# Every engine's instructions in program order, squares summed on POOL and gate rows combined on wide tiles, in a one-core mLSTM and convolution layer

## The chip, the cores and the metric

One core of a Trainium2 chip runs the whole kernel: TensorE (PE) for matmuls, VectorE (DVE), ScalarE (ACT), GpSimd (POOL), and SyncE (SP), which issues every DMA here. The metric is device microseconds of one execution. The version before takes 1819.15 us in the median of three runs (1818.57 to 1821.37).

## What is computed

One layer of a hybrid decoder, in float32, for 2048 tokens of width 1024:

```python
h = rms_norm(x, g_pre)
proj = jnp.einsum('bsd,de->bse', h, w_in)
q, k, v, o, z_m, i_pre, f_pre, u, gate_b, gate_c, z_c = jnp.split(
    proj, _split_points(), axis=-1)
...
log_i = i_pre + b_i
log_f = jax.nn.log_sigmoid(f_pre + b_f)
hm = mlstm_chunkwise(qh, kh, vh, log_i, log_f)
hm = group_rms_norm(hm, g_head, N_MLSTM_HEADS, x.dtype)
y_m = jax.nn.silu(z_m) * jax.nn.sigmoid(o) * hm
conv = causal_depthwise_conv(gate_c * u, conv_w)
y_c = jax.nn.silu(z_c) * group_rms_norm(gate_b * conv, g_conv, N_CONV_GROUPS, x.dtype)
out = jnp.einsum('bse,ed->bsd', jnp.concatenate([y_m, y_c], axis=-1), w_out)
return x + rms_norm(out, g_post)
```

There are 4 mLSTM heads with two gates each (`i_pre`, `f_pre`: eight columns of the projection) and 16 groups of convolution channels.

## The kernel before

**Precision by splitting.** A float32 operand is split in a high part, a rounded copy made on ACT (`split_h`, L165), and a low part, the difference made on DVE (`split_l`, L168). A product is high×high, high×low and low×high: three matmuls (L275 to L277).

**Products.** The sequence is worked in two halves of 1024 tokens. For a half, the output columns are 32 pairs of 128-column blocks, and each pair is a 2×2 block product (two column blocks by two 512-token quarters, over two halves of the channels) done with seven products in place of eight. The seven token operands, `hops[0]` to `hops[6]` (tiles `hH`, `hL`), are sums and differences of the normed input, built once a half. The seven weight operands of a pair (tile `w`) are made from four loaded blocks (`wraw`) by additions on DVE (L217, L241); those sums (`s`) are stored in DRAM (`w_scr`) and loaded again for the second half. A product is 4 × 3 = 12 matmuls into one 128x512 bank of PSUM. The banks of a pair are `uX`, `uD` and `uY`, filled in the order XDYXYDY; between the products ACT copies banks (`evac`, L434, L437, L440), and `TAKE` functions hand the results on: q, k and v through DRAM (`cs` L289, `tr` L295, `v_scr`), and the gates, convolution (`conv_0`), its group norm (`group_stat`, `rstd` on POOL, L391 and L392) and its output (`take_zz`).

**Slots.** A slot is one product. `on(slot, fn)` and `later(d, fn)` enter side work in an agenda; `run_slot` calls what stands there, bank copies first, then weights, stores and the rest. The weights of product i are planned in `plan_weights`: the load (`w_load`, on SP) 8 slots ahead, the sum (`w_sum`) 5, the cast (`w_high`) 4, the subtraction (`w_low`) 3. mLSTM work (`plan_group`) comes in groups of two chunks, 16 groups a half, about every 11 slots: an ACT and DVE chain from the PE results `num` and `upd` over `rd`, `numsb` (L698), its squares (L699), `rstd` on POOL and a last scaling (L704). What the agenda gives is the order in which the program is written. The order in which each engine runs its instructions is then set by the framework's scheduler, which may move them within their data dependencies.

**Start.** `start` does pairs 0 and 1 of the first half with plain products over eight channel blocks (`plain`, tiles `uH`, `uL`, made unnormed by L846 and L847), since the norm of the tokens isn't known yet. Meanwhile it sums the squares (`square` on ACT, L854; `sum_up` on PE with a matrix of ones, L860), takes root (L863) and reciprocal (L866) into `rb`, norms the blocks (`norm`, L871), scales the plain results (`plain_take`, L911), and builds the hops (`diff`, `fill`). Gate columns are done there by `gate_weights` (the tile `wgt`), `gate_proj` (L476) and `gate_take`, which adds high and low rows, multiplies by the norm and adds the bias on tiles of 4 partitions (L483, L489, L490, L491) and stores rows to DRAM. `plan_gates` loads them later as 128x32 tiles.

**End.** At the last slots `wo_hop` loads and splits the output weights into the hop tiles and `y_even` the first mix tile; then come 16 token tiles of the output projection (`po`, L593 to L595).

Of the kernel before, what the change touches and what calls it, by code (L numbers as in the profile page):

```python
# [16 lines left out]
P = 128  # L17
# [46 lines left out]
def hybrid_layer_kernel(  # L64
# [16 lines left out]

    const = ctx.enter_context(tc.tile_pool(name="const", bufs=1))
# [8 lines left out]
    graw_scr = scratch("graw_scr", [NH, HT])  # L91
# [32 lines left out]
    gb = const.tile([NH, 2], F32, name="gb")  # L124
# [27 lines left out]
    def t5(name, dtype=F32):  # L152
        return tpool.tile([P, Q], dtype, tag="t5", name=name)
# [128 lines left out]
    def seg(qd):  # L282
        return slice(Q * qd, Q * qd + Q)
# [196 lines left out]
    def gate_take(hf, qd, bank, scale=None):  # L480
        for w in range(2):
            lo_ = t5("glo")[0:NH]
            nc.vector.tensor_copy(lo_, bank[64 * w + 32 : 64 * w + 36])  # L483
            r = t5("grow")[0:NH]
            if scale is None:
                nc.vector.scalar_tensor_tensor(
                    r, bank[64 * w : 64 * w + NH], gb[:, w : w + 1], lo_, ALU.add, ALU.add)
            else:
# [5 lines left out]
    def plan_gates(hf, s):  # L494
        W32 = HT * NH // P
        wide = lambda a: a.rearrange("h (c q) -> (h c) q", q=W32)
        f, e, d, s2, pz = (
            sm.tile([P, W32], F32, tag="g" + n, name="g" + n, bufs=1) for n in ("f", "e", "d", "s2", "p"))
        R = {}

        def load():
            nc.sync.dma_start(f, wide(graw_scr[hf]))
# [80 lines left out]
        for d_, fn in (  # L583
            (0, load), (2, decay), (4, log1p_0), (5, lambda: log1p_1((13, 11))), (6, lambda: log1p_1((9, 7))),
            (7, log1p_2), (10, rows_load), (12, rows_0), (13, rows_1), (14, rows_2), (15, rows_3),
            (16, rows_4), (17, rows_5), (19, cols), (20, cols_take),
        ):
            on(s + d_, fn)
# [228 lines left out]
    def start():  # L817
# [32 lines left out]
        ssq = {}  # L850
# [14 lines left out]
        def inverse(qd):  # L865
            nc.vector.reciprocal(rb[:, seg(qd)], rb[:, seg(qd)])  # L866
# [35 lines left out]
        def plain(n, ch, qd):  # L902
            bank = bank_("u")
            for half in range(2):
                for k in range(KH):
                    plain_k(bank, n, ch, qd, half, k)
            return bank

        def plain_take(n, ch, qd, bank):
            t = t5("u")  # L910
            nc.vector.tensor_tensor(t, bank, rb[:, seg(qd)], ALU.mult)  # L911
            kind, i = PAIRS[n]
            TAKE[kind](0, i, ch, qd, t, False)
# [14 lines left out]
        nc.sync.dma_start(gb, gate_bias.rearrange("o (w h) -> h (o w)", w=2))  # L928
# [7 lines left out]
        for half in range(2):  # L936
            for k in range(KH):
                b = 2 * half
                unscaled(b, k)
# [5 lines left out]
                sum_up(0, KH * half + k, square(b, k))  # L945
            run_slot()
        for q in range(4):
            weights(1, q)
        root(0)
        inverse(0)  # L950
        p1 = [plain(1, 0, 0)]
        for k in range(KH):
            unscaled(1, k)
        for ch in range(2):
            plain_take(0, ch, 0, banks[ch])
        run_slot()
        gate_weights()
        sqs = [square(1, k) for k in range(KH)]
        p1.append(plain(1, 1, 0))
        norm(0)  # L960
        run_slot()
        for k in range(KH):
            unscaled(3, k)
            sqs.append(square(3, k))
        gate = gate_proj(((U[0], 0), (U[2], 1)))
        for i in range(KT):
            sum_up(1, i, sqs[i])
        run_slot()
        fill(0, 0)
        root(1)  # L970
        norm(2)
        for ch in range(2):
            plain_take(1, ch, 0, p1[ch])
        p0 = [plain(0, 0, 1)]
        run_slot()
        inverse(1)
        norm(1)
        gate_take(0, 0, gate, rb[:, seg(0)])
        p0.append(plain(0, 1, 1))
        norm(3)  # L980
# [4 lines left out]
        p1 = [plain(1, 0, 1)]  # L985
        for ch in range(2):
            plain_take(0, ch, 1, p0[ch])
        fill(3, 2)
        run_slot()
        fill(6, 3)  # L990
        diff(3, 3, 0)
        p1.append(plain(1, 1, 1))
        run_slot()
        diff(2, 2, 3)
        gate = gate_proj(((U[1], 0), (U[3], 1)))
        plain_take(1, 0, 1, p1[0])
        run_slot()
        plain_take(1, 1, 1, p1[1])
        gate_take(0, 1, gate, rb[:, seg(1)])
        run_slot()  # L1000
        fill(2, 3)
        run_slot()
        fill(4, 0)
        run_slot()
        fill(5, 2)
        run_slot()
# [6 lines left out]

    def load_wo(e, w2):
        for half in range(2):
            raw = t5("wor")
            nc.sync.dma_start(raw, wout[e * P : (e + 1) * P, seg(half)])
            split(w2[:, 0, seg(half)], w2[:, 1, seg(half)], raw)
        wos[e] = (w2[:, 0], w2[:, 1])

    def wo_hop(e):
        j, part = divmod(e, 2)
        load_wo(e, hpool.tile([P, 2, DM], F32R, tag=f"h{j}{'HL'[part]}", name="wo"))

    def load_y(t, tile_):
        hf, tt = divmod(t, NC)
        ts = slice(tt * P, (tt + 1) * P)
        ys[t] = []
        for g in range(2):
            H, L = tile_(f"yH{g}"), tile_(f"yL{g}")  # L1030
            for half in range(2):
                r = tpool.tile([P, 4, P], F32, tag="t5", name="yr")
                es = slice(4 * half, 4 * half + 4)
                if g == 0:
                    for i in range(2):
                        nc.sync.dma_start(
                            r[:, 2 * i : 2 * i + 2, :],
                            h_scr[hf][2 * half + i, tt].rearrange("e p t -> p e t"))
                    gr = tpool.tile([P, 4, P], F32, tag="t5", name="gr")
                    nc.sync.dma_start(gr, g_scr[hf][es, :, ts].rearrange("e p t -> p e t"))  # L1040
                    nc.vector.tensor_tensor(r, r, gr, ALU.mult)
                else:
                    nc.sync.dma_start(r, y_scr[hf][es, :, ts].rearrange("e p t -> p e t"))
                split(H[:, es], L[:, es], r)
            ys[t] += [(H[:, i, :], L[:, i, :]) for i in range(8)]

    def y_even(t):
        tags = iter(("cv", "cv", "cu", "rb"))
        load_y(t, lambda name: c4(next(tags), name, [P, 8, P], F32R))
# [3 lines left out]
    OZ0 = 24 * NPROD  # L1053
    plan_weights()
# [5 lines left out]
    plan_gates(0, 15)  # L1060
    plan_gates(1, U + 9)
# [42 lines left out]
    while any(agenda.values()):  # L1104
        run_slot()
    ph1.close()
# [105 lines left out]
```

## Time and profile before

| | before |
|---|---|
| median of 3 runs | 1819.15 us (1818.57 to 1821.37) |
| profiled execution, its own time | 1826.05 us |
| its span, first to last instruction | 1824.3 us |
| mean granted clock of TensorE | 0.987 |
| busy: PE, DVE, ACT, POOL | 1764.4, 1153.4, 817.5, 94.1 us |
| moved by DMA | 278.18 MB |

All durations below come from the one profiled execution. In the views, "[4.45 <-ACT w L165]" is idle time of the engine just before an instruction, and what ended it; PEclk or clock is the granted clock as a share of 2.4 GHz. An average over the span says little here: the start, the stretches with mLSTM work, the convolution and the output projection have different limits, so the windows are to be read one by one.

### The profile page before, as it was taken

Reading aid. Unit: us, or ns where it says so; the run is one execution under the profiler, and the core shown is the slowest. Engines: PE = TensorE matmul, PEld = TensorE weight load, DVE = VectorE, ACT = ScalarE, POOL = GpSimd, SP = SyncE. Lnnn points to the kernel's source line nnn. Section 1 sums busy time; section 2 is a strip of 40 time slices with the busy share of each in tenths; the row PEclk is TensorE's granted clock in tenths of the full one; section 3 lists DMA queues with packets and bytes.
Section 4 is the critical chain, followed back from the end, with each engine's and each line's share of the span. In section 5 each row is a group of like instructions: output and inputs, shape, how many; then the busy total and the mean of one; then the engine's idle time right before and its main releaser. Section 6 shows DMA issues by size and latency. Waiting matters only on the chain.

```text
span 1824.3 us, 23028 instructions
## 1 busy us (share of the span) xinstructions
PE 1764.4 (97%) x7801; PEld 1420.6 (78%) x7801; DVE 1153.4 (63%) x2193; ACT 817.5 (45%) x1599; POOL 94.1 (5%) x106
## 2 busy tenths in 40 slices
PE   8799889999999999999888999999999999999998
PEld 5577768888888878787666888888888888888887
DVE  7967459888878788844535867676756663333321
ACT  6334346655556555633334555564655541111110
POOL 0000001010101000000000101010100000000000
PEclk9999989999999999999999999999999999999999
DMA  6247557645455778656554545454455594334311
GB/s 209 43 127 181 132 153 219 194 152 160 138 168 164 209 242 267 220 144 157 137 123 128 152 122 151 115 152 122 136 156 145 179 298 147 115 116 120 111 53 40
DMA packets 358946, 278.18 MB, mean 152 GB/s; under 512 B 186724, under 2 KB 268908, under 8 KB 358828
## 3 DMA queue, kind: packets, MB, share of 16 engines
q1 hardware_dynamic: 358828, 276.71, 52.8%
q8 instruction: 61, 1.00, 0.2%
q14 instruction: 57, 0.47, 0.1%
HBM read 183.13 MB, written 93.49 MB: 152 GB/s over the span
## 4 chain that ended last, share of the span: by engine, by line
PE 79%; issue 12%; DMA 3%; DVE 3%; ACT 2%; SPq 1%; POOL 0%; DVEq 0%; ACTq 0%; POOLq 0%
PE uY L275 8%; PE uY L277 8%; PE uY L276 8%; PE po L594 7%; PE po L593 7%; PE po L595 6%; PE uX L277 5%; PE uX L275 5%; PE uX L276 5%; PE uD L275 5%; PE uD L277 5%; PE uD L276 5%; PE num L594 1%; PE num L595 1%; SPq L189 1%
## 5 line engine op out<-in xcount | busy, mean ns | idle before, releaser
L168 DVE TENSOR_TENSOR w<-wraw,w 128x512 fp32r<-128x512 f32 x410 | 279.0, 687 | 136.4 <-ACT w L165 135.4
L165 ACT CAST w<-wraw 128x512 fp32r<-128x512 f32 x410 | 249.9, 619 | 172.3 <-PE uY L277 81.8
L275 PE MATMUL uY<-hH,w 128*128 128x512 f32 x744 | 299.4, 402 | 21.3 <-ACT w L165 17.0
L277 PE MATMUL uY<-hH,w 128*128 128x512 f32 x744 | 297.0, 399 | 2.8 <-DVE w L168 2.8
L276 PE MATMUL uY<-hL,w 128*128 128x512 f32 x744 | 295.6, 397 | 0.0
L275 PE MATMUL uD<-hH,w 128*128 128x512 f32 x496 | 200.8, 405 | 11.8 <-ACT w L165 11.8
L275 PE MATMUL uX<-hH,w 128*128 128x512 f32 x496 | 199.2, 402 | 8.2 <-ACT w L165 8.2
L594 PE MATMUL po<-wo,yH 128*128 128x512 f32 (+1 forms) x528 | 205.5, 389 | 0.0
L593 PE MATMUL po<-wo,yH 128*128 128x512 f32 (+1 forms) x528 | 204.3, 387 | 0.0
L595 PE MATMUL po<-wo,yL 128*128 128x512 f32 (+1 forms) x528 | 203.7, 386 | 0.0
L277 PE MATMUL uD<-hH,w 128*128 128x512 f32 x496 | 200.5, 404 | 0.7 <-DVE w L168 0.7
L276 PE MATMUL uD<-hL,w 128*128 128x512 f32 x496 | 200.1, 403 | 0.0
L277 PE MATMUL uX<-hH,w 128*128 128x512 f32 x496 | 199.1, 401 | 0.8 <-DVE w L168 0.8
L276 PE MATMUL uX<-hL,w 128*128 128x512 f32 x496 | 198.4, 400 | 0.0
L275 PEld LDWEIGHTS uY<-hH,w 128*128 128x128 f32 x744 | 141.1, 190 | 59.1 <-ACT w L165 21.0
L277 PEld LDWEIGHTS uY<-hH,w 128*128 128x128 f32 x744 | 140.9, 189 | 40.1 <-DVE w L168 6.3
L276 PEld LDWEIGHTS uY<-hL,w 128*128 128x128 f32 x744 | 141.3, 190 | 31.9
L275 PEld LDWEIGHTS uD<-hH,w 128*128 128x128 f32 x496 | 95.5, 193 | 34.2 <-ACT w L165 12.6
L275 PEld LDWEIGHTS uX<-hH,w 128*128 128x128 f32 x496 | 94.4, 190 | 31.9 <-ACT w L165 10.5
L593 PEld LDWEIGHTS po<-wo,yH 128*128 128x128 f32 x528 | 99.2, 188 | 23.0 <-DVE c L449 0.4
L595 PEld LDWEIGHTS po<-wo,yL 128*128 128x128 f32 x528 | 99.2, 188 | 21.5
L594 PEld LDWEIGHTS po<-wo,yH 128*128 128x128 f32 x528 | 99.3, 188 | 20.9
(198 smaller groups left out, 2589.1 us busy)
## 6 DMA issues: line engine op xcount, KB each, us to landing
wraw<-in_wt_dram SPq DMA_DIRECT2D x226, 256.0 KB
wraw<-w_scr SPq DMA_DIRECT2D x120, 256.0 KB
w_scr<-wraw SPq DMA_DIRECT2D x90, 256.0 KB
v_scr<-tr SPq DMA_DIRECT2D x128, 64.0 KB
vraw<-v_scr SPq DMA_DIRECT2D x32, 256.0 KB
h_scr<-hT SPq DMA_DIRECT2D x128, 64.0 KB
y_scr<-sg SPq DMA_DIRECT2D x32, 256.0 KB
g_scr<-c SPq DMA_DIRECT2D x32, 256.0 KB
```

The source lines that it names most:

```text
L165: nc.scalar.copy(dH, src)
L168: nc.vector.tensor_tensor(dL, src, dH.bitcast(F32), ALU.subtract)
L189: later(d, lambda: nc.sync.dma_start(dst, src), STORE)
L275: nc.tensor.matmul(bank, wH[:, k, :], bH[:, k, :], start=first, stop=False, **kw)
L276: nc.tensor.matmul(bank, wH[:, k, :], bL[:, k, :], start=False, stop=False, **kw)
L277: nc.tensor.matmul(bank, wL[:, k, :], bH[:, k, :], start=False, stop=stop and k == KH - 1, **kw)
L593: nc.tensor.matmul(out_, aH, bH, start=start, stop=False)
L594: nc.tensor.matmul(out_, aH, bL, start=False, stop=False)
L595: nc.tensor.matmul(out_, aL, bH, start=False, stop=stop)
```

## The change

1. `in_order`, called at the end of every slot, chains each instruction to the one written before it on the same engine (PE, DVE, ACT, POOL, SP) by an order-only dependency. Through the two input halves each engine then runs what the agenda wrote, in that order. The output stage behind it isn't chained.
2. Squares: of 8 squared tiles of a quarter 7 are added on POOL (L889), and one ones-matmul follows (L893) where 8 stood.
3. Gate rows: `gate_take` copies the bank with ACT (L503) and stores four strips of 4 rows; `plan_gates` loads them as 128x32 tiles, together with the reciprocal norms (`r_scr`), and combines them there in a new step; later steps move by a slot or two.
4. `start` is written in another order: squares of the first quarter before the blocks of the second, `inverse` and `norm` earlier, `gate_weights` after the first hop, v's transposes put off to later slots, some differences from other blocks, and the last hops spread over more slots.
5. Output weights (`plan_wo`) and the first mix tile (`y_parts`) are loaded some slots before they are split, and spread over more slots.

```diff
+    def in_order(start=False):
+        ins = nc.cur_bb.bb.instructions
+        n = traced.pop("n", 0)
+        for i in ins[n:]:
+            if i.engine not in ENGINES:
+                continue
+            prev = traced.get(i.engine)
+            if prev is not None and not start:
+                tc.add_manual_dep(
+                    i, prev,
+                    mybir.DependencyInfo(mybir.DependencyClass.NoSync, mybir.DependencyReason.DATA),
+                    reason="in_order")
+            traced[i.engine] = i.name
+        traced["n"] = len(ins)
...
         clock[0] += 1
+        in_order()
...
-    def gate_take(hf, qd, bank, scale=None):
-        for w in range(2):
-            lo_ = t5("glo")[0:NH]
-            nc.vector.tensor_copy(lo_, bank[64 * w + 32 : 64 * w + 36])
...
-                nc.vector.tensor_tensor(r, bank[64 * w : 64 * w + NH], lo_, ALU.add)
-                nc.vector.tensor_tensor(r, r, scale[0:NH], ALU.mult)
-                nc.vector.tensor_scalar(r, r, gb[:, w : w + 1], None, ALU.add)
-            nc.sync.dma_start((graw_scr[hf] if w else gate_scr[hf][0])[:, seg(qd)], r)
+    def gate_take(hf, qd, bank):
+        t = t5("graw")[0:GW]
+        nc.scalar.copy(t, bank)
+        for i in range(4):
+            store(graw_scr[hf][i][:, seg(qd)], t[32 * i : 32 * i + NH])
...
+        def combine():
+            for w, t in enumerate((li, f)):
+                hi, lo = R["raw"][:, 2 * w], R["raw"][:, 2 * w + 1]
+                if scaled:
+                    nc.vector.tensor_tensor(t, hi, lo, ALU.add)
+                    nc.vector.tensor_tensor(t, t, R["r"], ALU.mult)
+                    nc.vector.tensor_scalar(t, t, gb[:, w : w + 1], None, ALU.add)
+                else:
+                    nc.vector.scalar_tensor_tensor(t, hi, gb[:, w : w + 1], lo, ALU.add, ALU.add)
+            store(wide(gate_scr[hf][0]), li)
...
             nc.scalar.activation(sq, raw(b, k)[:, 0], AF.Square)
-            return sq
-
-        def sum_up(qd, i, sq):
-            if i == 0:
-                ssq[qd] = ps.tile([P, Q], F32, tag="g", name="ssq")
-            nc.tensor.matmul(ssq[qd], ones, sq, start=i == 0, stop=i == KT - 1)
+            qd = b % 2
+            if qd not in acc:
+                acc[qd] = sq
+            else:
+                nc.gpsimd.tensor_tensor(acc[qd], acc[qd], sq, ALU.add)
+
+        def sum_up(qd):
+            ssq[qd] = ps.tile([P, Q], F32, tag="g", name="ssq")
+            nc.tensor.matmul(ssq[qd], ones, acc[qd], start=True, stop=True)
...
+        weights(1, 0)
+        weights(1, 1)
+        for half in range(2):
+            for k in range(KH):
+                square(2 * half, k)
+        weights(1, 2)
+        weights(1, 3)
+        run_slot()
+        for b in (1, 3):
+            for k in range(KH):
+                unscaled(b, k)
+        p1 = [plain(1, 0, 0, lambda: sum_up(0))]
         root(0)
         inverse(0)
+        norm(0)
+        for b in (1, 3):
+            for k in range(KH):
+                square(b, k)
+        run_slot()
+        p1.append(plain(1, 1, 0))
         for ch in range(2):
             plain_take(0, ch, 0, banks[ch])
+        norm(2)
+        fill(0, 0)
         gate_weights()
         run_slot()
         gate = gate_proj(((U[0], 0), (U[2], 1)))
+        sum_up(1)
+        gate_take(0, 0, gate)
         root(1)
+        inverse(1)
+        norm(1)
+        run_slot()
...
-    on(2 * U - 3 * NPROD, lambda: y_even(0))
-    for j in range(NPROD):
-        for part in range(2):
-            on(2 * U - NPROD + j + 1, lambda e=2 * j + part: wo_hop(e))
+    for i, (load, go) in enumerate(y_parts(0, even_tile())):
+        on(2 * U - 3 * NPROD + 2 * i, load)
+        on(2 * U - 3 * NPROD + 2 * i + 3, go)
+    for e in range(2 * NPROD):
+        plan_wo(e)
```

ACT, near the first two-chunk group of mLSTM work (about 200 us in the profile before). A row is line, operation and output and input tiles; "x4" is four in a row. Before:

```order
L289 COPY cs<-uY 128x512
L165 CAST cH<-state_112 128x258
L698 ACTIVATE numsb<-num,rd 128x256
L699 ACTIVATE num,hss<-numsb 128x256
L704 ACTIVATE numsb<-numsb,hss 128x256 x2
L165 CAST w<-s_1571 128x512
L434 COPY uY<-uX 128x512
L165 CAST w<-wraw 128x512 x4
```

The same place in the change (L185 is the cast of before's L165, L728, L729 and L734 are its L698, L699 and L704, L310, L455 and L461 its bank copies L289, L434 and L440):

```order
L185 CAST cH<-state_113 128x258
L728 ACTIVATE numsb<-num,rd 128x256
L729 ACTIVATE num,hss<-numsb 128x256
L653 ACTIVATE R<-R 128x256
L461 COPY u_1780<-uY 128x512
L185 CAST w<-wraw 128x512
L310 COPY cs<-uX 128x512
L185 CAST w<-s_1785 128x512
L185 CAST kH<-kT 128x256
L185 CAST qH<-tmp 128x256
L185 CAST w<-wraw 128x512
L734 ACTIVATE numsb<-numsb,hss 128x256 x2
```

Before, L704 stands right behind L699 and four weight casts are gathered further on; in the change three weight casts, one a slot, stand between L729 and L734.

DVE in the start, from the scaling of the first plain results to behind the second reciprocal. Before:

```order
L911 TENSOR_TENSOR u<-u,rb_164 128x512 x2
L483 COPY glo<-gate 4x512
L168 TENSOR_TENSOR hL_592<-xs,hH_591 128x1024
L489 TENSOR_TENSOR grow<-gate,glo 4x512
L483 COPY glo<-gate 4x512
L490 TENSOR_TENSOR grow<-grow,rb_164 4x512
L866 RECIPROCAL rb_164<-rb_164 128x512
L491 TENSOR_SCALAR grow<-grow,gb 4x512
```

In the change, from the first reciprocal on (L899 is before's L866, L904 its L871, L946 its L911, L188 its L168; L485 clears the gate weights):

```order
L899 RECIPROCAL rb_165<-rb_165 128x512
L904 SCALAR_TENSOR_TENSOR xs<-xs,gp,rb_165 128x512 x4
L946 TENSOR_TENSOR u<-u,rb_165 128x512 x2
L904 SCALAR_TENSOR_TENSOR xs<-xs,gp,rb_165 128x512 x4
L188 TENSOR_TENSOR hL_429<-xs,hH_428 128x1024 x2
L485 CAST wgt<-zero 128x800
L489 TENSOR_TENSOR wgt<-wgraw,wgt 128x8x4 x2
L899 RECIPROCAL rb_165<-rb_165 128x512
```

The operations on 4 partitions are gone, and the gate weights, which stood at the head of DVE's program and ahead of the first reciprocal, stand between the two reciprocals.

## Rows read from the trace of the kernel before

**Rows 1.** The page, busy time of each engine over the span.

```profile
PE 1764.4 (97%) x7801; PEld 1420.6 (78%) x7801; DVE 1153.4 (63%) x2193; ACT 817.5 (45%) x1599; POOL 94.1 (5%) x106
```

**Rows 2.** Windows: length, busy PE, PEld, DVE, ACT, POOL, clock, DMA share, GB/s.

```profile
45.60:91.20 45.60, 35.18 (x139) 25.87 (x137) 44.90 (x59) 13.71 (x19) 0.00 (x0) 0.92 0.21 43
100.00:270.00 170.00, 156.58 (x665) 124.78 (x664) 99.22 (x198) 63.37 (x124) 2.05 (x4) 0.95 0.60 155
195.00:210.00 15.00, 10.55 (x40) 8.36 (x39) 8.29 (x17) 6.78 (x15) 0.90 (x2) 0.77 0.39 109
270.00:600.00 330.00, 330.00 (x1518) 270.59 (x1517) 281.19 (x564) 194.87 (x384) 38.28 (x38) 1.00 0.56 168
600.00:760.00 160.00, 156.56 (x706) 126.79 (x705) 131.79 (x236) 96.47 (x179) 7.83 (x8) 1.00 0.79 246
840.00:1000.00 160.00, 141.32 (x593) 107.86 (x593) 71.71 (x151) 59.09 (x125) 2.66 (x6) 0.96 0.57 138
```

**Rows 3.** Waits of PE: waited for, total us, times, longest us.

```profile
PE uD L275 <- ACT w L165: 11.8, 3, 4.5
```

**Rows 4.** Timeline near 200 us: start, us, engine, line, operation, tiles, [idle before].

```profile
199.81 0.91 ACT L704 ACTIVATE numsb<-numsb,hss 128x256 f32<-128x256 f32 x2 [1.11 <-POOL hss L392]
200.63 0.60 ACT L165 CAST w<-s 128x512 fp32r<-128x512 f32 x1
201.28 0.79 PE L275 MATMUL uD<-hH,w 128*128 128x512 f32 x1 [4.45 <-ACT w L165]
```

**Rows 5.** Timeline near 940 us, ACT, and SP's queue.

```profile
940.20 0.58 ACT L289 COPY cs<-uY 128x512 f32<-128x512 f32 x1 [6.96 <-PE uY L277]
...
946.30 0.62 ACT L165 CAST w<-wraw 128x512 fp32r<-128x512 f32 x1
...
939.47 2.18 SPq L189 DMA_DIRECT2D v_scr<-tr  x4
```

**Rows 6.** Timeline of the start: blocks, squares, their sum, reciprocals, first product.

```profile
16.16 2.76 ACT L846 ACTIVATE uH<-xs,gp 128x512 fp32r<-128x512 f32 x4
18.83 4.26 ACT L854 ACTIVATE xsq<-xs 128x512 f32<-128x512 f32 x8
...
31.34 3.35 DVE L866 RECIPROCAL rb<-rb 128x512 f32<-128x512 f32 x1 [3.46 <-ACT rb L863]
...
42.30 7.03 PE L860 MATMUL ssq<-xsq,ones 128*128 128x512 f32 x16
...
50.09 3.35 DVE L866 RECIPROCAL rb<-rb 128x512 f32<-128x512 f32 x1 [0.31 <-ACT rb L863]
...
89.21 0.80 PE L275 MATMUL uY<-hH,w 128*128 128x512 f32 x1 [10.42 <-ACT w L165]
```

**Rows 7.** Groups by line, DVE, 30 to 100 us: count, busy us, mean ns, idle.

```profile
L168 DVE TENSOR_TENSOR hL<-xs,hH 128x1024 fp32r<-128x1024 f32 (+1 forms) x16 | 16.7, 1072 | 0.0
L871 DVE SCALAR_TENSOR_TENSOR xs<-xs,gp,rb 128x512 f32<-128x512 f32 x16 | 11.1, 739 | 0.0
...
L483 DVE COPY glo<-gate 4x512 f32<-4x512 f32 x4 | 2.7, 687 | 0.2
L489 DVE TENSOR_TENSOR grow<-gate,glo 4x512 f32<-4x512 f32 x4 | 2.7, 682 | 0.1
L490 DVE TENSOR_TENSOR grow<-grow,rb 4x512 f32<-4x512 f32 x4 | 2.7, 672 | 0.0
L491 DVE TENSOR_SCALAR grow<-grow,gb 4x512 f32<-4x512 f32 x4 | 1.7, 436 | 0.0
```

**Rows 8.** POOL: a group of the start, then the timeline around 307 us.

```profile
masks.py:199 POOL TENSOR_SCALAR_AFFINE_SELECT ident<-ident 128x128 f32<-128x128 f32 x1 | 0.3, 292 | 0.0
...
306.64 2.90 POOL L392 TENSOR_TENSOR red<-red,mhalf 128x16 f32<-128x16 f32 x1
307.89 0.68 DVE L217 TENSOR_TENSOR s<-wraw 128x512 f32<-128x512 f32 x1
```

**Rows 9.** The chain of waits, a weight load's landing.

```profile
607.05 5.91 DMA wraw<-in_wt_dram
```

More of the change, by code (lines that the diff above doesn't have):

```diff
@@ L90, in hybrid_layer_kernel @@
     g_scr = scratch("g_scr", [8, P, HT])
-    graw_scr = scratch("graw_scr", [NH, HT])
+    graw_scr = scratch("graw_scr", [4, NH, HT])
+    r_scr = dram.tile([HT], F32, name="r_scr")
     gate_scr = scratch("gate_scr", [2, NH, HT])
@@ L499, in plan_gates @@
         R = {}
         def load():
-            nc.sync.dma_start(f, wide(graw_scr[hf]))
+            R["raw"] = sm.tile([P, 4, W32], F32, tag="graw", name="graww", bufs=1)
+            for i in range(4):
+                nc.sync.dma_start(R["raw"][:, i], wide(graw_scr[hf][i]))
+            if scaled:
+                R["r"] = sm.tile([P, W32], F32, tag="gr", name="gr", bufs=1)
+                for h in range(NH):
+                    nc.sync.dma_start(R["r"][h * W32 : (h + 1) * W32], r_scr.rearrange("(c q) -> c q", q=W32))
@@ L900, in plain_k, with plain @@
             nc.tensor.matmul(bank, wL[:, k, :], bH[:, k, :], start=False, stop=end)
-        def plain(n, ch, qd):
+        def plain(n, ch, qd, between=None):
             bank = bank_("u")
@@ L906, in plain @@
                     plain_k(bank, n, ch, qd, half, k)
+                if half == 0 and between:
+                    between()
             return bank
@@ L912, in plain_take @@
             kind, i = PAIRS[n]
-            TAKE[kind](0, i, ch, qd, t, False)
+            slow = NSTART + 2 * ch + qd - clock[0] if kind == "v" else 0
+            later(slow, lambda: TAKE[kind](0, i, ch, qd, t, False))
         load(0, 0)
@@ L937, in start @@
             for k in range(KH):
-                b = 2 * half
-                unscaled(b, k)
+                unscaled(2 * half, k)
                 if k == 0:
@@ L944, in start @@
                     plain_k(banks[ch], 0, ch, 0, half, k)
[L945 to L948, printed above, removed]
+        weights(1, 0)
[10 more added lines that the diff above has]
+        p1 = [plain(1, 0, 0, lambda: sum_up(0))]
         root(0)
         inverse(0)
-        p1 = [plain(1, 0, 0)]
-        for k in range(KH):
-            unscaled(1, k)
+        norm(0)
[4 more added lines that the diff above has]
+        p1.append(plain(1, 1, 0))
         for ch in range(2):
             plain_take(0, ch, 0, banks[ch])
+        norm(2)
+        fill(0, 0)
+        gate_weights()
         run_slot()
[L957 to L960, printed above, removed]
-        run_slot()
[L962 to L971, printed above, removed]
+        gate = gate_proj(((U[0], 0), (U[2], 1)))
+        sum_up(1)
+        gate_take(0, 0, gate)
+        root(1)
+        inverse(1)
+        norm(1)
+        run_slot()
+        p0 = [plain(0, 0, 1)]
+        nc.sync.dma_start(r_scr.rearrange("(o t) -> o t", o=1), rb[0:1, :])
         for ch in range(2):
             plain_take(1, ch, 0, p1[ch])
-        p0 = [plain(0, 0, 1)]
+        norm(3)
         run_slot()
-        inverse(1)
-        norm(1)
-        gate_take(0, 0, gate, rb[:, seg(0)])
         p0.append(plain(0, 1, 1))
-        norm(3)
         diff(0, 1, 0)
@@ L1005, in start @@
         fill(5, 2)
+        run_slot()
+        fill(6, 3)
+        run_slot()
         run_slot()
@@ L1012, in hybrid_layer_kernel, with wo_raw, wo_split, plan_wo @@
     wos, ys = {}, {}
+    def wo_raw(e, half, raw=None):
+        raw = raw or t5("wor")
+        nc.sync.dma_start(raw, wout[e * P : (e + 1) * P, seg(half)])
+        return raw
+    def wo_split(e, half, w2, raw):
+        split(w2[:, 0, seg(half)], w2[:, 1, seg(half)], raw)
+        wos[e] = (w2[:, 0], w2[:, 1])
     def load_wo(e, w2):
         for half in range(2):
[L1016 to L1021, printed above, removed]
-        j, part = divmod(e, 2)
-        load_wo(e, hpool.tile([P, 2, DM], F32R, tag=f"h{j}{'HL'[part]}", name="wo"))
-    def load_y(t, tile_):
+            wo_split(e, half, w2, wo_raw(e, half))
+    def plan_wo(e):
+        s = 2 * U - NPROD + 1 + 3 * e // 4
+        j, part = divmod(e, 2)
+        R = {}
+        def load():
+            for half in range(2):
+                R[half] = wo_raw(e, half, rawp.tile([P, Q], F32, tag="raw", name="wor"))
+        def go():
+            w2 = hpool.tile([P, 2, DM], F32R, tag=f"h{j}{'HL'[part]}", name="wo")
+            for half in range(2):
+                wo_split(e, half, w2, R[half])
+        on(s - 2, load)
+        on(s, go)
+    def y_parts(t, tile_):
         hf, tt = divmod(t, NC)
@@ L1029, in load_y @@
         for g in range(2):
-            H, L = tile_(f"yH{g}"), tile_(f"yL{g}")
+            R = {}
             for half in range(2):
-                r = tpool.tile([P, 4, P], F32, tag="t5", name="yr")
                 es = slice(4 * half, 4 * half + 4)
[L1034 to L1044, printed above, removed]
@@ L1045, in load_y, with load @@
-            ys[t] += [(H[:, i, :], L[:, i, :]) for i in range(8)]
+                def load(g=g, half=half, es=es, R=R):
+                    r = R[half] = tpool.tile([P, 4, P], F32, tag="t5", name="yr")
+                    if g == 0:
+                        for i in range(2):
+                            nc.sync.dma_start(
+                                r[:, 2 * i : 2 * i + 2, :],
+                                h_scr[hf][2 * half + i, tt].rearrange("e p t -> p e t"))
+                        R["g", half] = tpool.tile([P, 4, P], F32, tag="t5", name="gr")
+                        nc.sync.dma_start(R["g", half], g_scr[hf][es, :, ts].rearrange("e p t -> p e t"))
+                    else:
+                        nc.sync.dma_start(r, y_scr[hf][es, :, ts].rearrange("e p t -> p e t"))
@@ new lines, in go @@
+                def go(g=g, half=half, es=es, R=R):
+                    if half == 0:
+                        R["H"], R["L"] = tile_(f"yH{g}"), tile_(f"yL{g}")
+                    r = R[half]
+                    if g == 0:
+                        nc.vector.tensor_tensor(r, r, R["g", half], ALU.mult)
+                    split(R["H"][:, es], R["L"][:, es], r)
+                    if half == 1:
+                        ys[t].extend((R["H"][:, i, :], R["L"][:, i, :]) for i in range(8))
+                yield load, go
@@ L1047, in y_even, with load_y, even_tile @@
+    def load_y(t, tile_):
+        for load, go in y_parts(t, tile_):
+            load()
+            go()
+    def even_tile():
+        tags = iter(("cv", "cv", "cu", "rb"))
+        return lambda name: c4(next(tags), name, [P, 8, P], F32R)
     def y_even(t):
-        tags = iter(("cv", "cv", "cu", "rb"))
-        load_y(t, lambda name: c4(next(tags), name, [P, 8, P], F32R))
+        load_y(t, even_tile())
     U = NPAIR * NPROD
     OZ0 = 24 * NPROD
+    in_order(True)
     plan_weights()
```

46 lines of the change are left out of this document (21 added, 25 removed).

## The prediction

> **What bounds the kernel now.** The table of busy time shows TensorE (PE) at 1764.4 of 1824.3 us [rows 1]: the kernel gains only where PE stands still or runs at the lower of its two clocks, or where PE work goes. The windows tell where [rows 2]. Idle is the window less PE's busy time; clock loss is (1 − granted clock) × window, 1.00 being the 2.4 GHz level.
> - 45.6 to 91.2 us, the start: DVE busy 44.90 of 45.60 us. PE waits for it.
> - 100 to 270: 13.4 us idle, clock 0.95, so 8.5 us more: 21.9.
> - 270 to 600: no loss, though DVE is busy 281.19 of 330 us.
> - 600 to 760: 3.4 idle.
> - 840 to 1000: 18.7 idle, clock 0.96, so 6.4 more: 25.1, with DVE and ACT less than half busy.
>
> So in the middle no engine is full, yet PE waits. The waits of PE name ACT's cast of a weight block (L165) [rows 3]: three times for the bank uD, 4.5 us the longest, and likewise for uX and uY. The timeline around 200 us shows how [rows 4]: the cast stands on ACT directly behind L704, which waits 1.11 us for POOL at the end of a long mLSTM chain; the cast of 0.60 us then runs with PE already standing, 4.45 us. Around 940 us it is another neighbour [rows 5]: ACT waits 6.96 us for PE's product (the copy L289), and a cast that product order needs soon runs at 946.30, behind copies. Both are matters of the order in which ACT was told to work. A wait also lowers the clock afterwards: 195 to 210 us holds 4.45 us idle and a mean clock of 0.77, (1 − 0.77) × 15 = 3.45 us. One such miss costs 7.9 us.
>
> **The change, part by part.**
>
> *Program order.* In the written program a weight block is loaded 8 slots before its product, summed 5, cast on ACT 4 and subtracted on DVE 3 slots before. A product is 12 matmuls; at 330.00 us for 1518 [rows 2], 0.22 each with some shorter ones among them, it takes 2.6 to 2.8 us. So a cast gets some 11 us of lead. The ACT rows in the order of the change show it: casts now stand between the mLSTM pieces and ahead of L734, the old L704. A delay of 1.11 or 2 us is then covered by the three products ahead. The cover is gone if ACT or DVE gets over 8 us behind. I expect that in neither stretch and recover 0.9 of 21.9 + 25.1: **−42.3**; the ends are 0.5 (half the misses were late data, not order) and 1.0. At 600 to 760 us DVE is busy 131.79 of 160 us, so I take half of 3.4: **−1.7** (0 to −3.4). What can be late next is DVE: in program order it can't fetch light work out of the next slot where a slot is heavy. The zz pairs (8) put two group statistics and gates in some slots, some eleven operations of L217's 0.68 us [rows 8], 7.4 us of DVE against a 2.8 us product. A PSUM bank is needed again two products later, 5.6 us; 7.4 − 5.6 is under 2, and the weight lead takes part of it. Between 0 and 8 × 1.8 = 14 us; DVE at 281.19 of 330 without loss [rows 2] is nearer the low end: **+3**.
>
> *Squares.* Before, 16 ones-matmuls of two passes a sum: 7.03 us of PE each [rows 6]. One matmul remains of 8, so 7.03 × 7/8 = 6.2 us of PE go twice, and 7 POOL additions come for each sum. PE's part lies in the DVE-bound start, so it counts through the chain root, reciprocal, norm. No row has POOL adding 128x512. Bounds: 0.68 us, DVE's time for that shape (L217); above, the POOL row of 128x128 with one input, 0.292, four times the size and two inputs at double: 2.3 [rows 8]. I take 4 × 0.292 = 1.2, nearest to the POOL row. Squares follow at 0.53 us (4.26 for 8). They began at 18.83; written ahead of the four blocks of L846 (2.76 for 4) and two of the casts (0.62) that preceded them, they begin 4.0 earlier, at 14.8 us. The last addition ends at 15.9 + 7 × 1.2 = 24.3, the matmul (0.9) at 25.2. The root on ACT stands behind those two casts and 8 blocks (6.8 us), until 25.8. So the first reciprocal starts at about 26.5 instead of 31.34. At 2.3 it is 15.9 + 16.1 + 0.9 + 0.7 = 33.6, 2.3 us later than before.
>
> The Trainium skill, "GPSIMD Engine Reference", section "3.1 Elementwise — side-by-side cycle accounting", gives an fp32 addition 1.96 times DVE's time and says to keep elementwise work on DVE; an estimate from it is 1.96 × 0.68 = 1.33 us, 25.2 in place of 24.3, still hidden behind the root's wait for ACT.
>
> *Gate rows.* The four-partition operations (16, at 2.7 + 2.7 + 2.7 + 1.7 = 9.8 us [rows 7]) cost as much as full tiles and leave DVE; two copies on ACT (0.58 like L289) and eight stores come, later a few 128x32 operations in slots with room. Four of the 16 stood before the second reciprocal, 12 behind it (7.1 us).
>
> *Start reordered.* Between the reciprocals DVE now has 3.35, 8 × 0.69 (L871), two scalings at 0.68, 2 × 1.04 (hL, 16.7 for 16 [rows 7]) and the fill of the gate weights, which stood at the program's head: 800 wide, 0.8 by the 1024 of hL. Sum 13.1, so these are ready at 39.6. Only then can PE do the gate projection (16 × 0.22) and, behind it, the sum (0.9), ACT the root (0.7): 44.7, or 49.1 if the wait drops the clock to half. DVE stands 5.1 to 9.5 us for this **new wait**, with the norm of the second quarter behind it. The second reciprocal comes 1.0 to 5.4 us earlier than 50.09. From there to the first product before: 39.1 us. Less 7.1 gate operations, less three transposes put off (2.0), plus two scalings (1.4) and three hL (3.1) that stood elsewhere: 34.5. The first product starts at 79.2 to 83.6 in place of 89.21 [rows 6]; the products after it still wait for DVE's low halves, one after the other, so I count half of 5.6 to 10.0: **−4** (+8 with POOL at 2.3, −7 at the best).
>
> *Output weights and mix tiles* are loaded slots ahead: nothing, in the cover of PE's own products (L593 to L595 lose nothing above).
>
> **Sum**, against the profiled 1826.05: −42.3 − 1.7 + 3 − 4 = −45.0, so 1781.0. The median of the runs shown stands 6.9 lower. PE's full-clock work can't differ between executions; stalls can, and the change removes most, so half of the 6.9 counts: 1781.0 − 3.4 = 1778.
>
> **Rivals.**
> - *Waits move.* Half of 47 us stays, as misses in heavy DVE slots and as late sums: 1826 − 23.5 − 4 + 3 = 1801, less 3 to 6.9: 1795 to 1812. For: DVE at 281.19 of 330. Against: 270 to 600 loses nothing.
> - *POOL stands in DVE's way.* If an addition on POOL held DVE's two-input operations for its whole length, the seven of the second sum would cost DVE up to 7 × 1.2 = 8.4 us and those of the first, beside less DVE work, some 3: start +7, not −4, so 1789. Against: while POOL's L392 ran 2.90 us at 306.64, DVE's two-input L217 took its normal 0.68 [rows 8], though POOL read only 16 columns. The Trainium skill, "SBUF — State Buffer", section "🔬 SBUF: two separate sides", has such pairs block each other for whole instructions; the row just named speaks against it, at a small POOL operand.
> - *Slower: SP's queue in program order.* A store waits for its data, and loads behind it wait too. In the qk and v pairs four v_scr stores took 2.18 us of issue [rows 5], up to 12 issues stand in a slot, and their transposes depend on PE. Load to sum is three slots, 8.4 us; a landing took 5.91 [rows 9]. It decides when a load is issued over 2.5 us late. Each miss costs 7.9; 14 such pairs missing once in every second give 7 × 7.9 = 55, against −45: 1826 + 10 − 7 = 1829, a loss. Against: one slot's issues lag 3 us at most by the row's 0.55 each, and the next slots catch up.
> - *The order changes little*, since ACT's waits were for data: about 1819.
>
> **How the numbers follow.** About 3.6 us (0.2%) is what a measurement can tell. Forecast 0.57 (1760 to 1795), waits move 0.16, POOL in the way 0.08, little changes 0.04, slower 0.15. Faster is the first three: 0.81. The range goes from 1760 (middle fully regained, start −7: 1826 − 50 − 7 − 6.9 = 1762) to 1813 and leaves out the last two, 0.19.
>
> **What would show it.** Right: PE idle under 3 us at 100 to 270 and 840 to 1000 and granted clock 1.00; no PE wait on the weight cast over 1 us after the start; L893 twice, in place of 32 passes; first reciprocal at 26 to 28 us, second at 45 to 50, with DVE idle ahead of it. Wrong: PE waiting for DVE in the zz pairs; SP issuing weight loads late; POOL additions over 2 us, or DVE operations longer beside them. The forecast is wrong as a whole if PE's idle sum stays over 40 us.

## The result and the profile after

The change takes 1779.57 us in the median of four runs (1776.88 to 1782.27), against 1820.06 for the version before (1818.57 to 1821.37): a ratio of 0.9778, 95% interval 0.976 to 0.9796, some 40 us faster. The profiled execution took 1780.39 us (before: 1826.05), with a span of 1778.5. In one of the experiments below, the one with the gate weights early, one execution of four, the profiled one, took 3466.91 us; its ratio is from the other three and it has no rows here.

The page's busy time and the windows of the changed kernel, with the columns of [rows 2]:

```profile
PE 1735.6 (98%) x7773; PEld 1408.5 (79%) x7773; DVE 1153.6 (65%) x2175; ACT 820.9 (46%) x1608; POOL 121.3 (7%) x120
```

```profile
45.60:91.20 45.60, 33.76 (x132) 25.09 (x132) 37.69 (x44) 14.92 (x20) 0.00 (x0) 0.87 0.21 54
100.00:270.00 170.00, 170.00 (x769) 138.10 (x768) 118.28 (x244) 75.79 (x148) 2.64 (x4) 1.00 0.73 187
270.00:600.00 330.00, 328.52 (x1504) 268.64 (x1503) 276.74 (x544) 191.06 (x378) 45.52 (x38) 1.00 0.54 165
600.00:760.00 160.00, 158.41 (x712) 127.31 (x712) 134.40 (x231) 94.16 (x172) 5.80 (x8) 1.00 0.77 244
840.00:1000.00 160.00, 160.00 (x736) 131.05 (x735) 99.53 (x205) 78.47 (x164) 12.14 (x12) 1.00 0.60 149
```

The two stretches that held most of the loss have none now: PE is busy 170.00 of 170 and 160.00 of 160 us, at a granted clock of 1.00 ([rows 2] had 156.58 at 0.95 and 141.32 at 0.96). Where before lost nothing, 270 to 600 us, 1.5 us of idle is new. The start is the other way round: in 45.6 to 91.2 us DVE, which was busy 44.90 of 45.60, now stands for 7.9 us, and PE's clock is 0.87 in place of 0.92. PE's waits say where (waited for, total us, times, longest):

```profile
PE gate L497 <- DVE wgt L489: 10.5, 1, 10.5
...
PE uX L296 <- ACT w L185: 5.0, 1, 5.0
PE uX L298 <- DVE w L188: 4.3, 1, 4.3
PE ssq L893 <- POOL xsq L889: 3.7, 1, 3.7
PE uY L296 <- ACT uY L455: 3.5, 3, 1.5
```

The waits for the weight cast that [rows 3] listed are gone behind 100 us; the one of 5.0 us that is left lies at 86 us, in the start. ACT's timeline around 200 us answers to [rows 4]: a weight cast of 0.62 us now follows the bank copy of its own slot, and ACT waits for PE, not PE for ACT.

```profile
197.34 0.57 ACT L455 COPY uY<-uX 128x512 f32<-128x512 f32 x1 [1.71 <-PE uX L298]
197.82 0.62 ACT L185 CAST w<-wraw 128x512 fp32r<-128x512 f32 x1
198.42 0.62 ACT L185 CAST vH<-vraw 128x512 fp32r<-128x512 f32 x1
201.22 0.59 ACT L458 COPY p<-uD 128x512 f32<-128x512 f32 x1 [2.18 <-PE uD L298]
201.70 0.62 ACT L185 CAST w<-wraw 128x512 fp32r<-128x512 f32 x1
```

Where the time went is seen best by counting products, which both programs do in the same number. A product here is twelve matmuls with a hop operand; the count begins behind the plain products of the start. The first matmul of the fifth product and that of the 289th, in before:

```profile
101.65 0.39 PE L275 MATMUL uY<-hH,w 128*128 128x512 f32 x1
...
1020.32 0.40 PE L275 MATMUL uD<-hH,w 128*128 128x512 f32 x1
```

The same two in the change:

```profile
104.71 0.40 PE L296 MATMUL uY<-hH,w 128*128 128x512 f32 x1
...
969.13 0.39 PE L296 MATMUL uD<-hH,w 128*128 128x512 f32 x1
```

So the start is **3.1 us longer**. The 289th product began at 1020.32 us and now begins at 969.13: 51.2 us earlier, so the stretch between gained 51.2 + 3.1 = **54.3**. The last product's last matmul stands 49.5 us earlier (1.7 lost again, mostly on two new waits of 1.4 and 0.4 us), the end of the span 45.8: **3.7 us lost** behind it, where PE waits 1.8 us for split output weights (L623 and L624) and its granted clock is 0.50 from 1431.3 to 1434.6 us. Sum: −54.3 + 3.1 + 1.7 + 3.7 = −45.8.

The start in rows of the changed kernel. DVE and POOL first, merged rows of the timeline; then PE:

```profile
22.27 9.46 DVE L877 SCALAR_TENSOR_TENSOR uL<-xs,gp,uH 128x512 fp32r<-128x512 f32 x8
31.65 3.34 DVE L899 RECIPROCAL rb<-rb 128x512 f32<-128x512 f32 x1
35.03 6.20 DVE L904 SCALAR_TENSOR_TENSOR xs<-xs,gp,rb 128x512 f32<-128x512 f32 x4
...
42.35 2.72 DVE L904 SCALAR_TENSOR_TENSOR xs<-xs,gp,rb 128x512 f32<-128x512 f32 x4
...
48.12 0.31 DVE L489 TENSOR_TENSOR wgt<-wgraw,wgt 128x32 fp32r<-128x32 f32 x2 [0.28 <-ACT wgt L488]
55.74 3.35 DVE L899 RECIPROCAL rb<-rb 128x512 f32<-128x512 f32 x1 [7.31 <-ACT rb L896]
...
16.04 10.80 POOL L889 TENSOR_TENSOR xsq<-xsq 128x512 f32<-128x512 f32 x7 [14.39 <-ACT xsq L884]
29.86 10.83 POOL L889 TENSOR_TENSOR xsq<-xsq 128x512 f32<-128x512 f32 x7 [3.02 <-ACT xsq L884]
...
48.48 0.75 PE L497 MATMUL gate<-uH,wgt 128*100 128x512 f32 x1 [10.50 <-DVE wgt L489]
```

The four xs operations at 35.03 take 6.20 us; the four at 42.35, behind POOL's last addition, 2.72. Single instructions show why:

```profile
16.04 1.30 POOL L889 TENSOR_TENSOR xsq<-xsq 128x512 f32<-128x512 f32 x1 [14.39 <-ACT xsq L884]
...
23.57 1.60 POOL L889 TENSOR_TENSOR xsq<-xsq 128x512 f32<-128x512 f32 x1
23.96 1.75 DVE L877 SCALAR_TENSOR_TENSOR uL<-xs,gp,uH 128x512 fp32r<-128x512 f32 x1
...
25.25 1.59 POOL L889 TENSOR_TENSOR xsq<-xsq 128x512 f32<-128x512 f32 x1
25.64 1.75 DVE L877 SCALAR_TENSOR_TENSOR uL<-xs,gp,uH 128x512 fp32r<-128x512 f32 x1
...
28.63 0.74 DVE L877 SCALAR_TENSOR_TENSOR uL<-xs,gp,uH 128x512 fp32r<-128x512 f32 x1
...
32.96 1.30 POOL L889 TENSOR_TENSOR xsq<-xsq 128x512 f32<-128x512 f32 x1
```

Alone, a POOL addition takes 1.30 us and a DVE operation 0.74. Side by side they alternate: the DVE operation at 23.96 ends (25.71) about 0.5 us after the POOL addition that began at 23.57 (25.17), the next addition begins at 25.25 and is 1.59 long, and so on. So each one's time contains a wait for the other, and a pair takes 1.68 us. The 1.30 us addition at 32.96 runs beside DVE's reciprocal, which has one input and takes its normal 3.34.

### The profile page after: what moved, and what is told of

Same layout as the page of the kernel before. It is cut to its first block, busy times and chain, and to the rows that moved or that the text cites. A ratio compares the mean times of both kernels' runs of the same rounds, so it can differ in the third digit from the quotient of the medians.

```text
span 1778.5 us, 23028 instructions
## 1 busy us (share of the span) xinstructions
PE 1735.6 (98%) x7773; PEld 1408.5 (79%) x7773; DVE 1153.6 (65%) x2175; ACT 820.9 (46%) x1608; POOL 121.3 (7%) x120
## 4 chain that ended last, share of the span: by engine, by line
PE 88%; DVE 6%; ACT 2%; DMA 2%; issue 2%; SPq 0%; DVEq 0%
PE uY L296 9%; PE uY L298 9%; PE uY L297 9%; PE po L624 6%; PE po L625 6%; PE po L623 6%; PE uX L298 6%; PE uX L297 6%; PE uX L296 6%; PE uD L296 6%; PE uD L297 6%; PE uD L298 6%; PE gate L497 1%; PE num L623 1%; PE num L625 1%
## 5 line engine op out<-in xcount | busy, mean ns | idle before, releaser
L185 ACT CAST w<-wraw 128x512 fp32r<-128x512 f32 x410 | 254.1, 621 | 234.8 <-PE uY L298 103.6
L188 DVE TENSOR_TENSOR w<-wraw,w 128x512 fp32r<-128x512 f32 x410 | 280.1, 687 | 88.3 <-ACT w L185 85.8
L624 PE MATMUL po<-wo,yH 128*128 128x512 f32 (+1 forms) x528 | 206.3, 391 | 0.9 <-DVE wo L188 0.9
L623 PE MATMUL po<-wo,yH 128*128 128x512 f32 (+1 forms) x528 | 204.3, 387 | 0.9 <-ACT wo L185 0.9
L296 PE MATMUL uD<-hH,w 128*128 128x512 f32 x496 | 197.7, 399 | 0.0
L298 PE MATMUL uD<-hH,w 128*128 128x512 f32 x496 | 196.5, 396 | 0.0
L623 PEld LDWEIGHTS po<-wo,yH 128*128 128x128 f32 x528 | 99.4, 188 | 24.4 <-ACT wo L185 1.7
L624 PEld LDWEIGHTS po<-wo,yH 128*128 128x128 f32 x528 | 99.6, 189 | 22.7 <-DVE wo L188 1.5
L298 PEld LDWEIGHTS uX<-hH,w 128*128 128x128 f32 x496 | 93.9, 189 | 27.8 <-DVE w L188 5.0
L296 PEld LDWEIGHTS uX<-hH,w 128*128 128x128 f32 x496 | 93.9, 189 | 27.2 <-ACT w L185 5.5
```

What stands on the lines that cost most here:

```text
L185: nc.scalar.copy(dH, src)
L188: nc.vector.tensor_tensor(dL, src, dH.bitcast(F32), ALU.subtract)
L623: nc.tensor.matmul(out_, aH, bH, start=start, stop=False)
L624: nc.tensor.matmul(out_, aH, bL, start=False, stop=False)
```

## The experiments

The theory: the time before 1000 us was lost because the scheduler had put weight casts behind other work on ACT; written order gives it back. In the start two new costs, POOL's additions in DVE's way and the late gate weights, eat what the gate rows free. Rivals: the other parts of the change give the gain; the additions do no harm; the start hides its changes.

**Without the order chain.**

```diff
-            if prev is not None and not start:
+            if False:
```

> The change with the order chain alone taken away, so that the scheduler orders each engine again; squares, gate rows, start and loads stay as changed. Theory 1 (the gain is the order of the weight casts on ACT): TensorE waits for the cast again at 100 to 270 us and 840 to 1000 us, idle there over 20 us together where the changed kernel has under 1, and the time is 1815 to 1835 us. Theory 2 (the gain comes from the other parts): idle there stays under 5 us, time 1780 to 1790 us.

Measured: 1819.53 us, ratio to before 0.9992 (0.9982 to 1.0003): without the order everything else is worth nothing together. The windows have the idle time back, 12.7 and 19.1 us, and the start isn't long: the fifth product begins at 100.94 us, with POOL's additions still there.

```profile
100.00:270.00 170.00, 157.33 (x670) 124.63 (x669) 103.11 (x210) 64.59 (x125) 2.42 (x4) 0.96 0.62 157
840.00:1000.00 160.00, 140.94 (x602) 107.15 (x601) 76.83 (x163) 62.49 (x132) 2.86 (x6) 0.99 0.60 147
```

**The order chain alone.** `in_order` in the kernel before, from the end of `start` on.

```diff
...
     start()
+    in_order(True)
+    traced['go'] = True
```

> The kernel before with the order chain alone, set behind the start; squares, gate rows, start and loads as before. Theory 1 (order alone gives the middle, and the changed start costs some 3 us): no wait of TensorE over 2 us behind 100 us, first products where before has them (101.65 us for the fifth product), time 1763 to 1772 us, faster than the change. Theory 2 (the spread loads and the wide gate rows are needed for program order to work): waits in the middle remain, 1785 us or more.

Measured: 1793.7 us, ratio 0.9845 (0.9819 to 0.9872); a miss for both theories' times. The middle came as expected: from the fifth to the 289th product it gains 54.0 us (104.55 and 969.20, against 101.65 and 1020.32). The start, which is before's, was 2.9 us longer in this execution: ACT waited 1.44 us for a first token load, and the first reciprocal came at 33.07 us in place of 31.34. The next experiment has the same start and its fifth product at 101.93, so a start's length can differ by some 2.6 us between two executions. Behind 1340 us 13 us of idle arise, where before has 0.1 and the change 2.2:

```profile
1340.00:1460.00 120.00, 106.74 (x445) 85.61 (x445) 70.98 (x125) 63.40 (x117) 2.26 (x4) 0.93 0.65 200
```

```profile
PE uY L296 <- ACT u L461: 6.0, 1, 6.0
PE uY L296 <- DVE c L466: 5.3, 2, 5.0
```

There the old code loads output weights and casts them in the same slot. In written order ACT waits for the load, with the next bank copy (L461) queued behind and PE waiting for that copy:

```profile
1409.29 0.62 ACT L184 CAST wo<-wor 128x512 fp32r<-128x512 f32 x1 [4.20 <-DMA wor<-in_wout_dram]
...
1412.44 0.58 ACT L461 COPY u<-uY 128x512 f32<-128x512 f32 x1
1413.07 0.80 PE L296 MATMUL uY<-hH,w 128*128 128x512 f32 x1 [5.96 <-ACT u L461]
```

**Order and spread loads.** The same kernel with `plan_wo` and `y_parts` of the change.

```diff
-    on(2 * U - 3 * NPROD, lambda: y_even(0))
...
+    for i, (load, go) in enumerate(y_parts(0, even_tile())):
+        on(2 * U - 3 * NPROD + 2 * i, load)
+        on(2 * U - 3 * NPROD + 2 * i + 3, go)
+    for e in range(2 * NPROD):
+        plan_wo(e)
```

> The kernel before with the order chain behind the start, and with the output weights and the first mix tile loaded ahead and spread as in the change; squares, gate rows and start as before. Theory 1 (with order alone the end lost some 16 us because loads and their casts stood in one slot, and the start is worth the same old or new): the waits behind 1340 us go, time 1776 to 1781 us, within 3 us of the change. Theory 2 (the end's waits have another cause): 1788 us or more.

Measured: 1778.08 us, ratio 0.9771 (0.9755 to 0.9786), the same as the whole change. The window of the end:

```profile
1340.00:1460.00 120.00, 116.78 (x510) 93.31 (x509) 74.18 (x131) 64.86 (x123) 2.26 (x4) 1.00 0.74 223
```

So order and spread loads are the gain; squares on POOL, gate rows and the new start are worth nothing net.

**The order chain on ACT alone.**

```diff
-    ENGINES = (nc.tensor.engine, nc.vector.engine, nc.scalar.engine, nc.gpsimd.engine, nc.sync.engine)
+    ENGINES = (nc.scalar.engine,)
```

> The change with the order chain on ACT alone; PE, DVE, POOL and SP are ordered by the scheduler. Theory 1 (the place of the weight casts among ACT's instructions is what cost the middle): idle of TensorE at 100 to 270 and 840 to 1000 us is under 3 us together, time 1775 to 1790 us. Theory 2 (the weight loads on SP or DVE's order cost it as well): over 10 us of idle remain there, time 1795 us or more.

Measured: 1772.87 us, ratio 0.9744 (0.9727 to 0.976), some 7 us below the whole change. 3.2 us of idle stay at 100 to 270 us, against the full chain's none (2.8 of it one wait), so the bound of 3 was just missed, and the time lies below the range given:

```profile
100.00:270.00 170.00, 166.81 (x743) 134.48 (x742) 117.04 (x242) 71.44 (x143) 5.42 (x4) 0.99 0.72 185
840.00:1000.00 160.00, 160.00 (x738) 130.96 (x737) 101.61 (x215) 78.90 (x164) 10.95 (x12) 1.00 0.62 160
```

The order of ACT is what cost the middle. Its advantage over the full chain lies mainly in the start (fifth product at 101.19 us in place of 104.71) and behind the last product, where 0.3 us is lost in place of 3.7.

**Additions on DVE.**

```diff
-                nc.gpsimd.tensor_tensor(acc[qd], acc[qd], sq, ALU.add)
+                nc.vector.tensor_tensor(acc[qd], acc[qd], sq, ALU.add)
```

> The change with the 14 additions of squares on DVE. Theory 1 (POOL's additions hold DVE's two-input operations, about 9 us): uL and xs operations take 0.66 to 0.75 us again in place of up to 1.78, the additions of the first sum fit into DVE's 3.5 us wait, the first reciprocal starts at 26 to 27 us in place of 31.65, the second at 51 to 52, time 1774 to 1777 us. Theory 2 (the longer DVE operations are not POOL's doing): DVE gets 9.5 us more work, the second reciprocal starts at 56 to 60 us, time 1781 to 1786 us.

Measured: 1779.1 us, ratio 0.9769 (0.9747 to 0.9791): no different from the change. DVE's groups from 14 to 46 us:

```profile
L889 DVE TENSOR_TENSOR xsq<-xsq 128x512 f32<-128x512 f32 x14 | 9.7, 692 | 1.5 <-ACT xsq L884 0.2
L877 DVE SCALAR_TENSOR_TENSOR uL<-xs,gp,uH 128x512 fp32r<-128x512 f32 x10 | 6.8, 747 | 0.0
L904 DVE SCALAR_TENSOR_TENSOR xs<-xs,gp,rb 128x512 f32<-128x512 f32 x8 | 5.5, 747 | 0.0
```

The mechanism held: with POOL silent, uL and xs operations are all at 747 ns on the mean. The times missed what was expected, since DVE now does the 9.7 us of additions itself. The reciprocals come at 28.57 and 54.68 us, 3.1 and 1.1 us earlier than in the change (26 to 27 and 51 to 52 were expected).

**Gate weights early.** Cleared at the program's head, made ahead of the first root.

```diff
...
+        gate_weights()
         p1 = [plain(1, 0, 0, lambda: sum_up(0))]
...
         fill(0, 0)
-        gate_weights()
```

> The change with the gate weights made earlier: cleared at the head of the program, written ahead of the first root. Theory 1 (the start is one DVE chain, and the wait for the gate weights stops it): TensorE's 10.5 us wait for the gate weights goes, DVE's 7.3 us wait before the second reciprocal too, which starts at 47 to 48 us, and the time falls by 7 to 9 us to 1771 to 1773 us. Theory 2 (behind the second reciprocal weight loads or PE hold the first products): the reciprocal comes earlier but the fifth product less than 3 us, time 1777 to 1780 us.

Measured: 1770.45 us in the median, ratio 0.9719 (0.9693 to 0.9744), 9 us below the change and a little below the range expected. The next experiment holds the same edit and has rows.

**Gate weights early, the first seven additions on DVE, the second seven on POOL.**

```diff
...
-                nc.gpsimd.tensor_tensor(acc[qd], acc[qd], sq, ALU.add)
+                (nc.gpsimd if qd else nc.vector).tensor_tensor(acc[qd], acc[qd], sq, ALU.add)
```

> The change with the gate weights made early, and the first sum's seven additions on DVE, where it waits for squares anyway; the second sum's stay on POOL. Theory 1 (one DVE chain, from which POOL's first seven additions take some 5 us and DVE's own 2 less than that): first reciprocal at 28 to 29 us, second at 43 to 46 us, time 1766 to 1769 us. Theory 2 (behind the gate weights another wait sets the start): second reciprocal at 47 us or later, time 1769 to 1772 us, no better than with early gate weights alone.

Measured: 1767.87 us, ratio 0.9715 (0.9699 to 0.9731). DVE's timeline:

```profile
16.04 5.46 DVE L889 TENSOR_TENSOR xsq<-xsq 128x512 f32<-128x512 f32 x7
...
29.25 3.34 DVE L899 RECIPROCAL rb<-rb 128x512 f32<-128x512 f32 x1
32.62 6.29 DVE L904 SCALAR_TENSOR_TENSOR xs<-xs,gp,rb 128x512 f32<-128x512 f32 x4
...
44.94 3.34 DVE L899 RECIPROCAL rb<-rb 128x512 f32<-128x512 f32 x1
```

DVE does not wait before the second reciprocal, which is 10.8 us earlier than in the change, and the fifth product starts at 92.95 us, 11.8 earlier; the time falls by as much, 11.7. PE's wait for the gate weights is gone too. Here, and with the gate rows put back below, the start behaves as one DVE chain: what leaves it leaves the total. The second sum's additions on POOL still hold the four xs operations (6.29 us).

**The gate rows put back.** The old operations on 4 partitions, as extra work on DVE.

```diff
     def gate_take(hf, qd, bank):
+        for w in range(2 if hf == 0 else 0):
+            lo_ = t5("glo")[0:NH]
+            nc.vector.tensor_copy(lo_, bank[64 * w + 32 : 64 * w + 36])
...
```

> The change with the 16 operations on 4 partitions put back on DVE as extra work in the start (their results are not used). Theory 1 (the start is DVE's chain, the gate rows were worth their 9.8 us nearly in full): the eight of the first quarter come between the gate projection and the second reciprocal and delay it by 3 to 4 us from 55.74, the other eight 4.9 us, the fifth product and the end come 7 to 9 us later, time 1786 to 1789 us. Theory 2 (they hide in DVE's wait): under 3 us, 1780 to 1782 us.

Measured: 1788.49 us, ratio 0.9831 (0.9811 to 0.985), 8.9 us above the change for 9.8 us of work. The first eight begin when the gate projection is done and end where the reciprocal starts:

```profile
53.88 0.68 DVE L504 COPY glo<-gate 4x512 f32<-4x512 f32 x1 [5.76 <-PE gate L497]
...
58.83 0.47 DVE L508 TENSOR_SCALAR grow<-grow,gb 4x512 f32<-4x512 f32 x1
59.40 3.35 DVE L906 RECIPROCAL rb<-rb 128x512 f32<-128x512 f32 x1
```

**All engines in order in the start, only ACT behind it,** on the best version so far.

```diff
     start()
+    traced['act'] = True
...
-            if i.engine not in ENGINES:
+            if i.engine not in (ENGINES if not traced.get('act') else (nc.scalar.engine,)):
```

> The version with early gate weights and the first additions on DVE, with all engines in program order in the start and only ACT behind it. Theory 1 (the start needs every engine in written order, the middle only ACT, and the 3.4 us lost behind the last product come from DVE's and SP's program order): the fifth product stays at 93 us, the middle as with full order, the last 3 us behind it come back, time 1763 to 1766 us. Theory 2 (DVE or SP must be in order in the middle too once the start is faster): waits of 1 to 4 us return there, 1768 us or more.

Measured: 1766.89 us, ratio 0.9704 (0.9691 to 0.9717), a little above the range expected. Behind the last product 0.9 us are lost in place of 3.4 in the version before it, but a wait of 2.8 us at 235 us returns, as with ACT alone. The intervals of this and the last version overlap; both beat the kernel before and the change.

## Why the prediction was right, and where its steps were not

The time, 1778 against 1779.57, came out right, and no rival's time came; the sum for the profiled execution was 1781.0 against 1780.39. That it came so near is luck: net of new waits, the order was to give 41.0 us and gave 52.6 (54.3 less the 1.7 lost again), the start was to give 4 and cost 3.1, the end was to cost nothing and cost 3.7. The errors cancel.

- *Program order: right, too small.* In the two stretches of [rows 2] nothing was late data: the share put at 0.9 was 1.0. From the fifth to the 289th product PE's idle time fell from 35.5 to 3.1 us and its clock loss (by the prediction's reckoning) from 15.4 to nothing, 47.8 together. The other 6.5 of the 54.3 lie within PE's busy time and were not counted at all. A matmul behind a wait is longer, 0.79 us in [rows 4] where its neighbours show 0.39 or 0.40, and before has 26 waits over 0.2 us there; that this is all of the 6.5 isn't shown. The run without the chain and the run with the chain alone show the gain of the order from both sides; ACT alone gives nearly all.
- *New waits, +3: right in size, by another mechanism.* Behind 100 us three waits of PE for the copy L455 make 3.5 us. Ahead of the two longest (1.5 and 1.4 us) ACT loads a function table twice (ACT_TABLE_LOAD), 1.28 us each time (at 305.07 and 306.81 us, and at 1245.57 and 1247.30), and the copy stands behind that in written order. DVE, on which the term was built, was waited for three times, 1.4 us in all, and no wait names a weight load; so the two rivals built on heavy DVE slots and on SP's queue did not come.
- *Start, −4: wrong, it was +3.1.* The step that failed is in "Squares": POOL's price was right (1.2 taken, 1.30 alone measured), but the additions were counted as work beside DVE. They held DVE's operations with two SBUF inputs: by 5.5 us up to the first reciprocal (two casts' low parts and four of the eight uL), by 3.5 behind it (four xs). The first reciprocal came at 31.65 us in place of 26.5, the second at 55.74 in place of 44.7 to 49.1; of the 4.6 us counted as gained behind it, 2.6 came. This was the second rival's mechanism, at 9.0 us where the rival had 8.4 + 3; the evidence held against it, one POOL row of 16 columns, could not carry that. Two of the prediction's own signs, the first reciprocal at 26 to 28 us and the second at 45 to 50, failed with it, and one of its signs of being wrong, longer DVE operations beside POOL's, came. Swapping the additions to DVE moved the time by nothing, since DVE's own 9.7 us replaced the 9.0.
- *Written order in the start* has a part in that too, which the prediction did not count. Without the chain the fifth product came at 100.94 us and with ACT alone in order at 101.19, in both with uL and xs operations of 1.74 to 1.78 us beside POOL. With ACT alone the second reciprocal stood at 55.71, as in the change, but DVE did other work ahead of it and waited 4.6 us in place of 7.3. As the starts of two executions can differ by 2.6 us, how much of the 3.1 is this stays open.
- *The new wait for the gate weights* was named and sized: DVE stood 7.3 us (5.1 to 9.5 predicted), PE 10.5. But it was accepted as part of the change's price; making those weights early was worth 9 us.
- *Gate rows, 9.8 us off DVE: right,* 8.9 when put back.
- *A row misread:* 89.21 us was called the first product. It is where PE's last long wait in the start ended; the first product had begun at 75.35. The count to the fifth product is the sound comparison.
- *Output weights, "nothing": wrong by both signs.* In written order 3.7 us are lost behind the last product, around PE's waits for the split weights (0.3 with ACT alone in order), and without the spread loads the order alone loses some 16 us (1793.7 against 1778.08).
- *Half of the 6.9 us* between profiled run and median was counted as stalls; the profiled execution of the change stands 0.8 above its median.

The Trainium skill, "SBUF — State Buffer", section "🔬 SBUF: two separate sides", states that a DVE operation with two SBUF inputs and a GpSimd operation that reads SBUF block each other. The trace agrees here, at 1.75 us for a DVE operation of 0.74 and 1.59 for a POOL addition of 1.30; the row that the prediction set against it, with 16 columns, did not show it. By the ratio of 1.96 to DVE's time in the Trainium skill, "GPSIMD Engine Reference", section "3.1 Elementwise — side-by-side cycle accounting", the addition was estimated at 1.33 us; 1.30 was measured.

## What to carry to other kernels

When no engine is full and the busiest one still waits, look at what stands directly ahead of the instruction that it waits for on that engine: an order written out by due times may beat a scheduler's, and one engine's order can be nearly all of it. Written order needs loads issued slots ahead of their use, since a wait then stops everything queued behind. Elementwise work moved to POOL isn't free for DVE: count some 1 us of DVE for each addition of full tiles (1.75 in place of 0.74 here) whenever DVE runs operations with two SBUF inputs beside it, unless a row with tiles of that size shows otherwise.

## What the runs showed of the hardware that was not expected

POOL and DVE took turns, instruction by instruction, for as long as both had two-input work of full tiles on SBUF: 128x512 additions alternating with uL operations at 1.68 us a pair, against 1.30 and 0.74 alone, which one after the other would be 2.04. A one-input reciprocal of 3.34 us beside them lost nothing, nor did a POOL addition beside it (1.30). POOL's operation on 128x16, 2.90 us long in [rows 8], held no DVE operation; where between the two sizes that changes isn't shown.
